# Other buffers for three leading MLP units, row-by-row differences of the activations, and block operands loaded product by product

## The chip, the cores and the metric

The program runs on one core of one Trainium2 chip. The metric is the device time of one launch in microseconds (us); the time of a kernel is the median of its runs. Before the change these were 3104.14, 3098.87 and 3105.69 us, median 3104.14 us. One more execution, taken by the hardware profiler, supplies every row shown here.

## The reference, cut to what matters

The network has two layers over 1024 latent tokens and 256 context tokens of 1024 channels in float32. Each layer has a mixer and then a squared-ReLU MLP, both under a modulated RMS norm:

```python
def squared_relu_mlp(h, w1, w2):
    return jnp.square(jax.nn.relu(h @ w1)) @ w2

x = x + mod_l[5] * squared_relu_mlp(modulate(rmsnorm(x, g_norm[l, 1]), mod_l[3], mod_l[4]), w_ff1[l], w_ff2[l])
return rmsnorm(x, g_final)
```

Only the MLP of the second layer is touched: `h` is 1024 tokens by 1024 channels, `w1` is 1024 by 4096, `w2` is 4096 by 1024. The context tokens have left the computation by then.

## The kernel before, in words

Precision first. A float32 operand is split into a high part `hi` (a cast on ACT, the scalar engine) and a low part `lo = v - hi` (a subtraction on DVE, the vector engine). A product is three matmuls, hi·hi, hi·lo and lo·hi, into one PSUM bank. So each 128x512 operand needs one ACT cast and one DVE subtraction before PE, the tensor engine, can use it. `osplit` (L1208 to L1217) makes the pair for an activation; L1265 and L1266 make it for a weight.

Both matmuls of this MLP are done by a seven-product scheme of the Strassen-Winograd kind. The operands are cut into 2 by 2 blocks, the blocks are added and subtracted, and seven products, named "1" to "7", take the place of eight. One **unit** computes a 2 by 2 group of 128x512 output tiles. The order of the products in a unit is `WORDER = ("1", "5", "6", "3", "7", "2", "4")`.

A unit has three PSUM banks (`BANK`, L1318): bank "a" (tag `acc`, 3 buffers) takes products 1, 6, 7 and 4 one on top of the other; bank "b" (tag `bd`, 4 buffers) takes 5 and then 3; bank "d" (also tag `bd`) takes 2. Between two products that accumulate in one bank, the running sum has to be copied out, because each of the four output tiles wants a different partial sum. So product 6 may start only when ACT has copied bank "a" after product 1 (`keep("11")`, line L1367), and product 7 only when the sum after 6 is copied (`keep("12")`). Product 2's bank is read by `plus("11")` (DVE, L1374, then ReLU and square on ACT, L1376 and L1377), which needs `keep("11")` done.

The up half (`h @ w1`): 16 units. The first three, `lead`, are **leading units** (`early=True`). Their products 1 and 2 need only the first 512 tokens, and run while the output projection of the mixer still finishes the other 512. Products 5, 6, 3, 7 and 4 need differences between the two halves of the tokens or the channels. These are made in `right1` (L1230 to L1251) once the norm of the second half is known. Then the five products are run for the three units together, one 128-row step of the inner dimension after the other (`together`). The twelve units 3 to 14 follow one by one, and unit 15 in another order.

The buffers around this: tag `x`, 8 buffers of 128x512, holds the residual stream of the first half, `x[k, 0]`, until `right1` has read it, and the output tiles of the units. `right1` releases its `x[k, 0]` of the lower channels only in its last loop (L1249, L1250), which forms the operand of product 4. Tag `t`, 5 buffers, holds sums of squares and temporaries. Tag `o`, 21 buffers, holds 16 operand tiles of products 6 and 7 throughout the up half, and on top of them `hi` parts on their way to DRAM. After a unit, `store` forms the right operands of the down half (differences of its four tiles) and writes them to `sw` in DRAM.

The down half (`... @ w2`): the hidden dimension is taken in five blocks, `DBLK`, of 2, 3, 3, 3 and 3 pairs of rows. Per block four units (`fo` = 0, 2, 4, 6), so with a 3-pair block a unit is 7 products x 3 steps x 3 matmuls = 63 matmuls, with the 2-pair block 42. The right operands of a block are loaded from `sw` by `down_ops` (L1419 on): 18 transfers of 256 KB straight into `hi` and `lo` tiles for products 1, 5 and 6 of a 3-pair block (L1430, tag `a5`, 32 buffers), and 12 into `t` tiles for 3, 7, 2 and 4 (L1433), which ACT and DVE then split into tiles of tag `a5` (product 3) or `o` (7, 2, 4). The left operands, weights, come per unit through staging tiles `st` (3 buffers) and `ws` (1 buffer), L1306, and are split by L1265 and L1266: first those of 1 and 2 (when the unit is made), then those of 5 and 6, of 3, and of 7 and 4 (when the unit meets product 5). Each result is added to the residual stream on DVE (L1442).

All transfers named here are issued by the SP queue, in order. The order of the instructions on each engine isn't written by hand: a scheduler runs through the program in a model of the chip, and at each moment gives an engine the ready instruction that comes first in program order (those under `tc.high_priority()` before). Readiness includes a free buffer. On the chip the order is fixed, and an engine waits at the head of its list.

Of the kernel before, what the change touches and what calls it, by code (L numbers as in the profile page):

```python
# [9 lines left out]
F32 = mybir.dt.float32  # L10
F32R = mybir.dt.float32r
# [6 lines left out]
P = 128  # L18
D = 1024
KT = D // P  # L20
# [31 lines left out]
def trunk(tc, es, A, out):  # L52
# [12 lines left out]
    def f(ap):  # L65
        return ap.bitcast(F32)
# [1141 lines left out]
    def osplit(pl, tag, bufs, v, b=None):  # L1208

        hi, lo = (pl.tile([P, 512], F32R, tag=tag, bufs=bufs, name=tag) for _ in range(2))  # L1210
        if b is None:
            act.copy(hi, v)
            dve.tensor_sub(lo, v, f(hi))
        else:
            act.activation(hi, v, AF.Identity, bias=b)
            dve.scalar_tensor_tensor(lo, v, b, f(hi), ADD, SUB)
        return hi, lo  # L1217
# [6 lines left out]
    def shift(k):  # L1224
        return mod[:, 1, 3, k, 0:1]
# [6 lines left out]
    def right1(r):  # L1232

        x, d = res.x, {}
        for k in range(HK):
            scaled(k, 1, r)
            dve.tensor_sub(x[k, 0], x[k, 1], x[k, 0])
        B["5"] = [osplit(ap_, "a5", 32, x[k, 0]) for k in range(HK)]
        for k in range(HK):
            scaled(k + HK, 1, r)  # L1240
            dve.tensor_sub(x[k, 0], x[k + HK, 1], x[k, 0])
        B["6"] = [osplit(po_, "o", NO, x[k, 0], shift(k + HK)) for k in range(HK)]
        B["3"] = [osplit(ap_, "a5", 32, x[k + HK, 1], shift(k + HK)) for k in range(HK)]
        db = pf.tile([P, 16], F32, name="db")[:, 0:HK]
        dve.tensor_sub(db, mod[:, 1, 3, HK:KT, 0], mod[:, 1, 3, 0:HK, 0])
        for k in range(HK):
            dve.tensor_sub(x[k, 1], x[k + HK, 1], x[k, 1])
        B["7"] = [osplit(po_, "o", NO, x[k, 1], db[:, k:k + 1]) for k in range(HK)]
        for k in range(HK):  # L1249
            dve.tensor_sub(x[k + HK, 0], x[k + HK, 0], x[k, 0])  # L1250
        B["4"] = [osplit(ap_, "a2", 8, x[k + HK, 0]) for k in range(HK)]  # L1251

    def left(load, n, early=False):
# [104 lines left out]
    def up_unit(j, early=False, order=WORDER):  # L1358

        t = {}  # L1360

        def e(n):
            t[n] = f(px.tile([P, 512], F32, tag="x", bufs=8, name="x"))
            return t[n]

        def keep(n):
            return lambda ps: act.copy(e(n), ps)  # L1367

        def square(n):
            dve.scalar_tensor_tensor(t[n], t[n], 0.0, t[n], MAX, MUL)  # L1370

        def plus(n):
            def g(ps):
                dve.tensor_add(t[n], t[n], ps)  # L1374
                if n == "11":
                    act.activation(t[n], t[n], AF.Relu)  # L1376
                    act.activation(t[n], t[n], AF.Square)  # L1377
                else:
                    square(n)
            return g  # L1380

        def last(ps):
            act.activation(e("21"), ps, AF.Relu)

        x5, x7 = (plus, keep) if order is LORDER else (keep, plus)
        done = {"1": keep("11"), "5": x5("22"), "6": keep("12"), "3": plus("12"), "7": x7("22"), "2": plus("11"),
                "4": last}
        u = Unit(up_left(j, early), done, B)

        def store():  # L1390
            act.activation(t["21"], t["21"], AF.Square)
            if j >= NWP:
                for n in ("11", "12", "21", "22"):
                    sp.dma_start(sd[2 * (j - NWP) + int(n[0]) - 1, int(n[1]) - 1], t[n])
                return

            def new(a, b):
                v = px.tile([P, 512], F32, tag="t", bufs=5, name="t")
                dve.tensor_sub(v, a, b)
                return v  # L1400

            o = {"1": t["11"], "2": t["21"], "3": t["22"]}
            o["5"] = new(t["12"], t["11"])
            o["6"] = new(t["22"], o["5"])
            dve.tensor_sub(t["12"], t["22"], t["12"])
            o["7"] = t["12"]
            o["4"] = new(t["21"], o["6"])
            for i, op in enumerate(WORDER):
                v = o[op]
                if i < NSPLIT:  # L1410
                    hi = po_.tile([P, 512], F32R, tag="o", bufs=NO, name="o")
                    act.copy(hi, v)
                    sp.dma_start(f(sw[j, i, 0]), f(hi))
                    dve.tensor_sub(v, v, f(hi))
                sp.dma_start(f(sw[j, i, 1]), v)
        u.store = store
        return u
# [84 lines left out]
    for i, blk in enumerate(DBLK):  # L1502
        right, nxt = nxt, {}
        for fo in range(0, KT, 2):
            if i or fo:
                d = down_unit(blk, fo, right)
            if i == 0 and fo < KT - 2:
                reload_x(fo + 2)
            if fo == KT - 2 and i + 1 < len(DBLK):
                nxt = down_ops(DBLK[i + 1])  # L1510
            d.run(*WORDER)
    s4, w4 = {}, []
    for hd in range(4):
        w4.append(wload(A["ff2"][1, 2 * NWP + hd], (1024,), *((None, "wa") if hd % 2 else (pfw, "wb"))))
# [103 lines left out]
```

## Time and profile before

| | before |
|---|---|
| median of the runs | 3104.14 us (3098.87 to 3105.69) |
| the profiled execution's own time | 3095.96 us |
| its span | 3094.2 us |
| PE busy, share of the span | 2933.4 us, 95% |
| DVE, ACT busy | 1959.3 us (63%), 1205.1 us (39%) |
| PE busy in 2400 to 2500 us, in 2700 to 2800 us | 79.64 and 89.24 of 100 us |
| mean granted TensorE clock of the span | 0.981 of full speed |

Where nothing else is said, times in the text are us from the start of the span. The MLP of the second layer takes the span from about 2400 us to its end; its down half begins at about 2740 us. [...]

### The profile page before, as it was taken

To read this page: it belongs to the slowest core of one execution; us is meant where nothing else is said; L and a number is where in the kernel's file an instruction comes from. 1 tells how busy PE (TensorE), PEld (TensorE's weight loads), DVE (VectorE), ACT (ScalarE), POOL (GpSimd) and SP (SyncE) were. 2 spreads that over 40 slices of the span, in tenths; PEclk is the share of its full clock that TensorE was granted. 3 is DMA by queue.
4 is the path that set the end of the run, shared out by engine and by line. 5 is a ranking of instruction groups with operands and counts; after the bars stand their busy time and mean duration, and the time that the engine had idled before them with its cause. 6 is when DMAs were issued, how large, how long until landed. Compare 5 with 4: busy or idle time off the path is not lost.

```text
span 3094.2 us, 44658 instructions
## 1 busy us (share of the span) xinstructions
PE 2933.4 (95%) x16386; PEld 2461.5 (80%) x16386; DVE 1959.3 (63%) x3885; ACT 1205.1 (39%) x2660; POOL 306.0 (10%) x483
## 2 busy tenths in 40 slices
PE   6899999999999999999999799999999799989998
PEld 5787878788888888888888677877877578867787
DVE  6859696646456544544446788567567776657666
ACT  3335354433321222222233145566666454433332
POOL 0002011001122222222100000000000000000000
PEclk9999999999999999999999899999999899999999
DMA  6143334551244444444321333232613386697751
GB/s 214 45 155 108 111 115 136 175 180 55 96 150 158 157 151 141 170 157 164 129 83 63 112 108 109 80 89 82 197 60 109 110 275 233 231 306 236 240 178 65
DMA packets 303803, 443.52 MB, mean 143 GB/s; under 512 B 25712, under 2 KB 174816, under 8 KB 303584
## 3 DMA queue, kind: packets, MB, share of 16 engines
q1 hardware_dynamic: 300992, 436.74, 43.4%
q10 hardware_dynamic: 2592, 3.93, 0.4%
q8 instruction: 129, 2.11, 0.3%
q14 instruction: 90, 0.74, 0.1%
HBM read 330.08 MB, written 110.49 MB: 142 GB/s over the span
## 4 chain that ended last, share of the span: by engine, by line
PE 73%; DVE 11%; DMA 9%; POOL 2%; ACT 2%; issue 2%; SPq 1%; POOLq 0%; DVEq 0%; ACTq 0%
PE acc L131 11%; PE acc L129 11%; PE acc L130 11%; PE acc L1314 8%; PE bd L1314 6%; PE ff L129 4%; PE ff L130 4%; PE ff L131 4%; PE po L1112 3%; PE S L1086 3%; DMA st<-in_ff_dram 2%; DMA kd<-rh 2%; PE pT L1107 2%; DMA qd<-rh 1%; DMA t<-sw 1%
## 5 line engine op out<-in xcount | busy, mean ns | idle before, releaser
L129 PE MATMUL acc<-a,wah 128*128 128x512 f32 (+1 forms) x1752 | 650.1, 371 | 22.4 <-DVE rt L1038 14.1
L130 PE MATMUL acc<-a,wah 128*128 128x512 f32 (+1 forms) x1752 | 644.6, 368 | 0.0
L131 PE MATMUL acc<-a,wal 128*128 128x512 f32 (+1 forms) x1752 | 643.4, 368 | 0.0
L129 PEld LDWEIGHTS acc<-a,wah 128*128 128x128 f32 x1752 | 336.0, 192 | 72.2 <-DVE rt L1038 14.7
L131 PEld LDWEIGHTS acc<-a,wal 128*128 128x128 f32 x1752 | 336.0, 192 | 47.5 <-DVE wal L111 0.6
L130 PEld LDWEIGHTS acc<-a,wah 128*128 128x128 f32 x1752 | 336.2, 192 | 45.6 <-issue 0.5
L110 ACT CAST wah<-st 128x1024 fp32r<-128x1024 f32 (+4 forms) x129 | 120.4, 935 | 483.2 <-DMA st<-in_ff_dram 375.1
L129 PE MATMUL ff<-s,wbh 128*128 128x512 f32 (+1 forms) x768 | 274.3, 359 | 0.2 <-DVE x L710 0.2
L130 PE MATMUL ff<-s,wbh 128*128 128x512 f32 (+1 forms) x768 | 272.4, 355 | 0.0
L131 PE MATMUL ff<-s,wbl 128*128 128x512 f32 (+1 forms) x768 | 271.6, 354 | 0.0
L111 DVE TENSOR_TENSOR wal<-st,wah 128x1024 fp32r<-128x1024 f32 (+4 forms) x129 | 139.3, 1083 | 202.9 <-ACT wah L110 202.6
L710 DVE SCALAR_TENSOR_TENSOR x<-ff,mod,x 128x512 f32<-128x512 f32 (+1 forms) x264 | 171.0, 658 | 96.1 <-PE ff L131 94.8
L1088 DVE TENSOR_REDUCE mx<-S 128x1 f32<-128x512 f32 (+1 forms) x288 | 165.6, 594 | 68.8 <-PE S L1086 67.3
L1094 ACT ACTIVATE p<-S,nm 128x512 f32<-128x512 f32 (+1 forms) x288 | 176.0, 620 | 45.7 <-DVE nm L1091 45.4
L1086 PE MATMUL S<-K,Q 128*128 128x512 f32 (+1 forms) x576 | 164.6, 386 | 15.7 <-ACT p L1094 7.1
L753 DVE TENSOR_TENSOR s<-s,s 128x512 fp32r<-128x512 f32 (+1 forms) x96 | 64.7, 680 | 167.9 <-ACT s L752 167.8
L1314 PE MATMUL bd<-a,wbh 128*128 128x512 f32 x480 | 153.9, 401 | 15.6 <-ACT wbh L1265 8.5
L129 PE MATMUL acc<-wah,a 128*128 128x256 f32 (+1 forms) x560 | 161.8, 290 | 6.5 <-ACT a L271 4.1
L129 PEld LDWEIGHTS ff<-s,wbh 128*128 128x128 f32 x768 | 144.8, 189 | 24.5 <-DVE x L710 1.0
L130 PEld LDWEIGHTS ff<-s,wbh 128*128 128x128 f32 x768 | 145.2, 189 | 20.7 <-DVE s L753 0.6
L131 PEld LDWEIGHTS ff<-s,wbl 128*128 128x128 f32 x768 | 144.9, 189 | 20.8
L131 PE MATMUL acc<-wah,a 128*128 128x256 f32 (+1 forms) x560 | 159.6, 290 | 0.3 <-DVE a L272 0.2
(391 smaller groups left out, 5913.1 us busy)
## 6 DMA issues: line engine op xcount, KB each, us to landing
st<-in_ff_dram SPq DMA_DIRECT2D x168, 256.0 KB
st<-in_ff_dram SPq DMA_DIRECT2D x68, 512.0 KB
st<-in_w_mod_dram SPq DMA_DIRECT2D x48, 512.0 KB
a<-sw SPq DMA_DIRECT2D x84, 256.0 KB
stm<-in_w_mod_dram SPq DMA_DIRECT2D x128, 128.0 KB
su<-st SPq DMA_DIRECT2D x32, 512.0 KB
bc<-rb SPq DMA_DIRECT2D x30, 512.0 KB
sv<-st SPq DMA_DIRECT2D x28, 512.0 KB
```

Of the source, the lines that this page charges most:

```text
L110: act.copy(hi, v)
L111: dve.tensor_sub(lo, v, f(hi))
L129: pe.matmul(ps, lh, rh, start=first, stop=False)
L130: pe.matmul(ps, lh, rl, start=False, stop=False)
L131: pe.matmul(ps, ll, rh, start=False, stop=last)
L710: dve.scalar_tensor_tensor(xt, ps, mod[:, self.l, ch, fo, s:s + 1], xt, MUL, ADD)
L753: dve.tensor_sub(lo, r, f(hi))
L1086: pe.matmul(s_, Q[m][:, kind, qb * P:(qb + 1) * P], K[hh, m][:, a:a + n], start=(kind == 0), stop=(kind == 1))
L1088: dve.tensor_reduce(mx[:, i:i + 1], s_, AX, MAX)
L1094: act.activation(e[:, a:a + n], S[i], AF.Exp, bias=nm, accum_out=Z[:, m, i:i + 1])
L1112: pe.matmul(po[:, 0:P], aT[:, (c - c0) * P:(c - c0 + 1) * P], v[c][:, hh * P:(hh + 1) * P], start=(c == 0), stop=(c == NCH - 1))
L1314: pe.matmul(ps, l_, r_, start=bool(first) and j == 0 and i == 0, stop=j == n - 1 and i == 2, skip_group_check=True)
```

## The change

Three things, in the order of the diff. In `right1`, the subtraction that forms the operand of product 4 for row `k` (old L1250) is put right behind the making and the split of that row's operand of product 6, in one loop. In `up_unit`, a leading unit puts the copy of product 1 ("11") into a `t` buffer and the copy of product 5 ("22") into an `o` buffer; "12" and "21", and all tiles of later units, stay in `x`. In the main loop, at the last unit of each block but the last, the remaining weights of that unit are asked for first, then the first unit of the next block is made and all its weights are asked for, and then the products run one by one, each followed by the loads of the next block's right operand for the same product; before, all loads of the next block stood ahead of the whole last unit. The number of computing instructions and of transfers is the same.

```diff
@@ -1239,15 +1239,14 @@
         for k in range(HK):
             scaled(k + HK, 1, r)
             dve.tensor_sub(x[k, 0], x[k + HK, 1], x[k, 0])
-        B["6"] = [osplit(po_, "o", NO, x[k, 0], shift(k + HK)) for k in range(HK)]
+            B["6"] = B.get("6", []) + [osplit(po_, "o", NO, x[k, 0], shift(k + HK))]
+            dve.tensor_sub(x[k + HK, 0], x[k + HK, 0], x[k, 0])
...
-        for k in range(HK):
-            dve.tensor_sub(x[k + HK, 0], x[k + HK, 0], x[k, 0])
         B["4"] = [osplit(ap_, "a2", 8, x[k + HK, 0]) for k in range(HK)]
@@ -1360,7 +1359,12 @@
         def e(n):
-            t[n] = f(px.tile([P, 512], F32, tag="x", bufs=8, name="x"))
+            if early and n == "11":
+                t[n] = px.tile([P, 512], F32, tag="t", bufs=5, name="t")
+            elif early and n == "22":
+                t[n] = f(po_.tile([P, 512], F32R, tag="o", bufs=NO, name="o"))
+            else:
+                t[n] = f(px.tile([P, 512], F32, tag="x", bufs=8, name="x"))
             return t[n]
@@ -1502,13 +1506,21 @@
         for fo in range(0, KT, 2):
-            if i or fo:
+            if fo:
                 d = down_unit(blk, fo, right)
...
-            if fo == KT - 2 and i + 1 < len(DBLK):
-                nxt = down_ops(DBLK[i + 1])
-            d.run(*WORDER)
+            last = fo == KT - 2 and i + 1 < len(DBLK)
+            if last:
+                next(d.left)
+                dn = down_unit(DBLK[i + 1], 0, nxt)
+                next(dn.left)
+            for op in WORDER:
+                d.run(op)
+                if last:
+                    nxt.update(down_ops(DBLK[i + 1], (op,)))
+            if last:
+                d = dn
```

## Rows read from the trace of the kernel before

**Rows 1.** The page: busy time of each engine (share of the span, instructions), and the chain of work that ended last, by engine.

```profile
PE 2933.4 (95%) x16386; PEld 2461.5 (80%) x16386; DVE 1959.3 (63%) x3885; ACT 1205.1 (39%) x2660; POOL 306.0 (10%) x483
...
PE 73%; DVE 11%; DMA 9%; POOL 2%; ACT 2%; issue 2%; SPq 1%; POOLq 0%; DVEq 0%; ACTq 0%
```

**Rows 2.** Busy time by stretch: bounds and length in us, then busy us and number of instructions of PE, PE's weight loads, DVE, ACT and POOL, then the granted TensorE clock, the share of the 16 DMA engines and GB/s.

```profile
2400.00:2500.00 100.00, 79.64 (x311) 59.76 (x311) 73.08 (x114) 47.73 (x77) 1.02 (x1) 0.88 0.44 142
2700.00:2800.00 100.00, 89.24 (x376) 70.93 (x375) 59.78 (x88) 38.89 (x65) 0.00 (x0) 0.95 0.88 290
```

**Rows 3.** PE in order of time around the five products of the leading units: start, length, line, output and inputs, and in brackets the idle time before and what ended it.

```profile
2429.72 0.65 PE L1314 MATMUL bd<-a,wbh 128*128 128x512 f32 x1 [2.75 <-ACT a L1212]
2432.79 0.80 PE L1314 MATMUL bd<-a,wbh 128*128 128x512 f32 x1 [2.42 <-DVE a L1213]
...
2449.29 1.22 PE L1314 MATMUL acc<-o,wbh 128*128 128x512 f32 x2 [11.88 <-ACT x L1367]
...
2482.73 0.73 PE L1314 MATMUL acc<-o,wah 128*128 128x512 f32 x2 [1.00 <-ACT x L1367]
```

**Rows 4.** Busy time by stretch (columns as in rows 2) of the same place.

```profile
2432.80:2437.40 4.60, 4.60 (x11) 3.06 (x11) 4.60 (x8) 1.64 (x3) 0.00 (x0) 0.57 0.00 0
2437.40:2449.30 11.90, 0.02 (x2) 0.01 (x1) 11.90 (x20) 6.19 (x11) 0.00 (x0) 0.62 0.00 0
2449.30:2454.10 4.80, 4.80 (x11) 3.26 (x12) 4.80 (x9) 4.62 (x9) 0.00 (x0) 0.53 0.02 5
2454.10:2465.40 11.30, 11.30 (x51) 9.24 (x50) 4.46 (x7) 5.70 (x12) 0.00 (x0) 1.00 0.18 46
```

**Rows 5.** DVE in order of time in `right1`.

```profile
2432.05 0.68 DVE L1213 TENSOR_TENSOR a<-x,a 128x512 fp32r<-128x512 f32 x1
...
2443.48 0.74 DVE L1216 SCALAR_TENSOR_TENSOR o<-x,mod,o 128x512 fp32r<-128x512 f32 x1
...
2447.88 0.68 DVE L1250 TENSOR_TENSOR x<-x 128x512 f32<-128x512 f32 x1
...
2449.74 0.68 DVE L1374 TENSOR_TENSOR x<-x,bd 128x512 f32<-128x512 f32 x1
```

**Rows 6.** ACT in order of time at the same place, with the last square of the norm's sum ahead of it.

```profile
2420.51 0.63 ACT L212 ACTIVATE t<-a 128x512 f32<-128x512 f32 x1
...
2448.65 0.58 ACT L1367 COPY x<-acc 128x512 f32<-128x512 f32 x1 [1.18 <-DVE x L1250]
...
2450.46 0.63 ACT L1376 ACTIVATE x<-x 128x512 f32<-128x512 f32 x1
```

**Rows 7.** PE in order of time in the down half, the rows that begin with an idle time: one from the last unit of the first block, three from the first two units of the second block, and four at the later changes of block.

```profile
2783.49 1.22 PE L1314 MATMUL bd<-a,wbh 128*128 128x512 f32 x2 [8.47 <-ACT wbh L1265]
...
2794.35 0.73 PE L1314 MATMUL acc<-o,wah 128*128 128x512 f32 x2 [0.83 <-DVE a L1442]
...
2802.23 0.70 PE L1314 MATMUL bd<-a,wbh 128*128 128x512 f32 x2 [0.52 <-DVE a L1442]
...
2815.91 0.73 PE L1314 MATMUL acc<-a,wbh 128*128 128x512 f32 x2 [1.01 <-DVE x L1442]
...
2876.85 0.73 PE L1314 MATMUL bd<-a,wbh 128*128 128x512 f32 x2 [0.67 <-DVE a L1442]
...
2919.17 0.72 PE L1314 MATMUL acc<-a,wbh 128*128 128x512 f32 x2 [0.85 <-DVE x L1442]
...
2936.83 0.74 PE L1314 MATMUL bd<-a,wbh 128*128 128x512 f32 x2 [0.76 <-DVE a L1442]
...
2987.85 0.71 PE L1314 MATMUL acc<-o,wah 128*128 128x512 f32 x2 [0.96 <-DVE a L1442]
```

**Rows 8.** Busy time by stretch (columns as in rows 2): after the gap at the first change of block, and one undisturbed unit of the second block.

```profile
2783.50:2788.40 4.90, 4.90 (x12) 3.81 (x13) 3.54 (x6) 2.92 (x6) 0.00 (x0) 0.51 0.91 286
...
2826.30:2840.70 14.40, 14.40 (x64) 11.84 (x64) 8.32 (x11) 3.04 (x5) 0.00 (x0) 1.00 0.34 96
```

**Rows 9.** The SP queue in order of time at the first change of block: start and length of a run of issues, line, destination and source, number of transfers.

```profile
2758.57 9.53 SPq L1430 DMA_DIRECT2D a<-sw  x16
2768.41 0.32 SPq L1433 DMA_DIRECT2D t<-sw  x1
2774.12 0.79 SPq L1430 DMA_DIRECT2D a<-sw  x2
2774.97 2.32 SPq L1433 DMA_DIRECT2D t<-sw  x5
2777.33 1.09 SPq L1306 DMA_DIRECT2D ws<-sv  x2
```

**Rows 10.** ACT in order of time there.

```profile
2774.82 0.62 ACT L1212 CAST a<-t 128x512 fp32r<-128x512 f32 x1 [10.37 <-PE acc L1314]
2780.56 2.00 ACT L1212 CAST o<-t 128x512 fp32r<-128x512 f32 x3 [5.12 <-DMA t<-sw]
2782.82 0.62 ACT L1265 CAST wbh<-ws 128x512 fp32r<-128x512 f32 x1 [0.26 <-DMA ws<-sv]
```

**Rows 11.** Busy time by stretch (columns as in rows 2) while the operands of the second block arrive.

```profile
2758.50:2768.30 9.80, 9.80 (x44) 8.02 (x44) 7.51 (x12) 2.17 (x4) 0.00 (x0) 1.00 1.01 343
2758.50:2783.10 24.60, 16.52 (x72) 13.17 (x71) 14.36 (x21) 4.92 (x9) 0.00 (x0) 0.90 0.86 296
2783.10:2795.50 12.40, 11.18 (x37) 8.41 (x38) 9.29 (x16) 6.41 (x12) 0.00 (x0) 0.79 0.96 284
```

## The prediction

> **What bounds the kernel.** I read the page first, then busy time by stretch, then PE's own order of time in the weak stretches, then ACT, DVE and SP there. PE is busy 95% of the span and makes 73% of the chain that ended last [rows 1]: with the number of matmuls unchanged, only PE's idle time and the time at its lower clock can be won. The change touches the second MLP, so the question is how much of either lies there. Two stretches of 100 us stand out: 2400 to 2500 us with 79.6 us of PE and a clock of 0.88, and 2700 to 2800 us with 89.2 us and 0.95 [rows 2]. In the first, PE waits 2.75 us, 2.42 us and then 11.88 us around the products 5 and 6 of the leading units [rows 3]; in the second it waits 8.47 us once, within the last unit of the first block [rows 7]. After both waits the clock is at its lower level for 4.8 to 4.9 us [rows 4, 8]. These two places are what the change can win; at the three later changes of block only four waits of 0.67 to 0.96 us are left [rows 7].
>
> As the unit of work I use 14.40 us for the 63 matmuls of an undisturbed unit [rows 8], 0.2286 us each.
>
> **Part 1: the leading units.** The 11.88 us end with the copy L1367 on ACT, `keep("11")` [rows 3], and this copy had waited for DVE's L1250 [rows 6], the last loop of `right1`, at 2447.88 us [rows 5]. So: product 1 stands in its bank, the copy needs an `x` buffer, all eight hold the residual stream, and the first one comes free with L1250. Product 6 may not accumulate before the copy; and product 5 of the second and third unit finds no `bd` bank, since product 2 sits in three of the four until `plus("11")`, DVE's L1374 at 2449.74 us, has run [rows 5].
>
> With "11" in `t` and "22" in `o`, copy, sum, ReLU and square run as soon as product 2 is done, before the norm. Then product 5 of all three units can follow the first rows, which are ready at 2432.05 us and after [rows 5], and PE goes on where it now stops at 2437.40 us [rows 4]. What is late next? The five products are 5 x 36 = 180 matmuls for the three units. Eleven are done by 2437.40 us [rows 4]; the other 25 of product 5 take 25 x 0.2286 = 5.7 us, to 2443.1. Product 6 takes its fourth row 27 matmuls later, at 2449.3. DVE now finishes that row at 2443.48 + 0.74 = 2444.2 us [rows 5]. The four subtractions moved ahead of it cost at most 4 x 0.68 = 2.7 us, so 2446.9: in time by 2.4 us. Without this cover the whole 2.7 us would be PE's. The copies of "12" need three `x` buffers when product 6 ends, about 2451.3; in the new order they come free row by row by then. Left where it is, the loop gives its first buffer at 2447.88 + 0.68 us [rows 5] and the others behind it, with the splits of product 7 between them: for the third buffer that is, as an estimate, 1 to 2 us too late. The reordering by itself is worth no more. Product 3, 7 and 4 come 8.2 us apart, their rows behind DVE work that the same queue does earlier than PE needs it.
>
> So 11.88 us go. The second start at the lower clock goes as well: 11 matmuls took 4.80 us [rows 4] where 11 x 0.2286 = 2.51 would do, 2.29 us. The wait of 1.00 us at 2482.73 us [rows 3] is again for an `x` buffer; the three units ask for 6 of the 8 in place of 12, so I let it go. The 2.75 and 2.42 us stay, they wait for the split of the first row.
>
> [...]
>
> Costs. Three copies of 0.58 us and six ReLUs and squares of 0.63 us [rows 6] move ahead of the norm on ACT, and DVE's three sums with them. ACT has idle time there (48 of 100 us busy [rows 2]), but a trio just ahead of the last square of the norm's sum [rows 6] would delay everything by 0.58 + 2 x 0.63 = 1.84 us. The squares now have one `t` buffer left of five, so each waits for the addition before it, at most 0.63 us more. Between 0 and 2.5 us, I take 0.5, near the idle end. In `store`, `o` has 21 - 16 - 3 = 2 buffers for high parts in place of 5, and three `t` are held. The cover is that "11" can be stored early and that unit 3 runs four products before it needs an `x` back; without it I bound the price by three waits of the 1.00 us kind, 3 us, and take 0.
>
> Part 1: -11.88 - 2.29 - 1.00 + 0.5 = -14.7 us.
>
> **Part 2: changes of block.** The 8.47 us end with the cast of weights of products 5 and 6 [rows 7]. Their transfer (`ws`) was issued at 2777.33 us, behind 18 + 6 loads of the next block [rows 9]: 16 went out at once, then SP stood from 2768.7 to 2774.1 us at a load whose `a5` buffer the last unit's own product 1 had to free, and five `t` loads went first as well. ACT was in the same position: a cast of a next-block operand waited 10.37 us, another three 5.12 us, with the weight cast behind them [rows 10]. With the unit's weights asked for before the block's operands, `ws` goes out when its buffer is free, well before 2774. Then the gap goes, and with it the slow restart: 12 matmuls in 4.90 us [rows 8] in place of 2.74, 2.16 us.
>
> What is late next is the operands themselves. Product 1 of the last unit ends at 2774.9; the other six are 36 matmuls, 8.2 us, so the next block starts at 2783.1 and its product 4, the last, at 2783.1 + 54 x 0.2286 = 2795.4. Until that time the DMA engines now move 24.6 x 296 + 12.4 x 284 = 10.8 MB from 2758.5 on [rows 11]; at the best rate seen, 343 GB/s, that is 31.5 us, to 2790.0. It fits by 5.4 us, and part of it is for later units. But twelve operands pass through five `t` buffers, and SP and ACT are in order. So some waiting comes back: between 0 and the whole 8.47 us. I take two waits of the mean length at later changes, 2 x 3.24 / 4 = 1.6 us [rows 7]. The waits of 0.83, 0.52 and 1.01 us behind the gap I leave.
>
> At the three later changes weights get ahead of operands too, but the four waits there, 3.24 us, are for DVE, and nothing says that they end: 0, with 3.24 either way. The gain could only come from the queue, and the queue isn't late there.
>
> Part 2: -8.47 - 2.16 + 1.6 = -9.0 us.
>
> **The sum.** -14.7 - 9.0 = -23.7 us. The profiled execution took 3095.96 us (span 3094.2, 1.8 us around it), so 3072.3 us for such an execution. It lies 8.2 us below the median shown, 3104.14; the change is to be seen against the median, so I forecast 3104.14 - 23.7 = 3080.4 us.
>
> **Rivals.** (a) Only the first stall goes: the block's operands are late in place of the weights, and the 8.47 us come back under another name. For it: the DMA engines are 86% and 96% busy there [rows 11]. Against: the 5.4 us of room. 3104.14 - 14.7 = 3089.4 us.
>
> (b) Only the second goes: DVE is busy for the whole 11.9 us of the first gap [rows 4], so PE could wait for rows of operands in place of banks. Against: rows of product 6 done at 2444.2 us. 3104.14 - 9.0 = 3095.1 us.
>
> (c) Slower: at the later changes a cast of an operand, whose buffer only the last unit's product frees, now stands on ACT right between the last unit's products and ahead of weight casts of the next unit. That is the mechanism of the 5.12 us in rows 10, at three places where it doesn't stop PE now. At the full price of the first change, 8.47 + 2.16 = 10.63 us each, it costs 31.9 us against 23.7: 3112.3 us. It decides from 7.9 us per change on. Against it: today's order puts these loads even earlier, and PE isn't stopped there.
>
> [...]
>
> (d) Nothing: the order on the engines comes from a planner that goes by readiness, and both stalls return with the same releasers. 3104 us. Against: in the first the buffer itself changes; in the second it is priority that decides between ready loads.
>
> **Chances and range.** Forecast 0.66, (a) 0.14, (b) 0.10, (c) 0.05, (d) 0.05. The forecast's own range is 3069 to 3088 us: with every wait named above gone (3.24 + 2.36 + the 1.6 and 0.5 I gave back, 7.7 us) and a median at the lowest of the runs shown it would be near 3068; with 2.5 + 3 + 2.7 us of uncovered cost, 3088. With (a) and most of (b): 3068 to 3097 us. About 0.2% (6.2 us) is what a measurement of this kernel can tell from no change. Faster by more: 0.66 + 0.14 and half of (b), 0.85; within: the rest of (b) and (d), 0.10; slower: 0.05.
>
> **What would show it.** Right: no idle time over 1 us between 2433 and 2460 us, L1367 of the leading units before the norm's reciprocal, the clock at its lower level once there; the five products done near 2476 us; `ws` issued ahead of most loads of the second block, no gap in the last unit of the first block. Wrong: PE waiting for L1216 or L1213 in product 6 (rival b), for a `t` cast in product 3, 7, 2 or 4 of the second block (a), gaps over 2 us at the later changes (c), or the old releasers with the old lengths (d).

## The result, and the profile after

The changed kernel takes 3079.69 us (median of 4 runs, 3076.41 to 3087.28) against 3103.01 us for the kernel before, run beside it. The ratio is 0.9928, with a 95% interval of 0.9909 to 0.9947: faster by 23.3 us, where 23.7 us were forecast. The two parts did not come out as forecast, though: the leads gave less and the changes of block more, and the two errors nearly cancel.

Up to the leads' first copies, at about 2394 us, PE, ACT and DVE run the same instructions in the same order in both programs, and still the leads' first landmark, the broadcast of the norm (L232), starts at 2425.84 us before and at 2431.91 us after. In the experiments below it lies between 2428.7 and 2439.0 us. So single profiles are compared over stretches that begin there:

- the **lead stretch**, from L232 to the ReLU of "21" of unit 7: before 163.79 us, after 153.24 us, 10.55 us less;
- from there to the 8th residual update of the down half: 166.63 and 166.80 us, no change;
- the **block stretch**, from that 8th update to the end of the span: before 337.94 us, after 322.75 us, 15.19 us less.

Of the kernel before, busy time by stretch (columns as in [rows 2]): the lead stretch, then the block stretch cut at the 28th update, which stands at the end of the first block.

```profile
2425.84:2589.63 163.79, 145.49 (x607) 115.41 (x608) 115.97 (x166) 81.00 (x127) 0.00 (x0) 0.94 0.57 195
...
2756.26:2796.35 40.09, 29.99 (x118) 23.41 (x119) 26.50 (x41) 11.70 (x21) 0.00 (x0) 0.87 0.89 290
2796.35:3094.20 297.85, 282.03 (x1315) 231.67 (x1313) 200.04 (x307) 86.96 (x135) 2.61 (x3) 0.99 0.56 176
```

The same of the kernel after, and the two stretches of [rows 2]:

```profile
2431.91:2585.15 153.24, 145.21 (x607) 115.36 (x608) 114.73 (x164) 77.56 (x121) 0.00 (x0) 0.97 0.60 208
...
2751.95:2780.08 28.13, 26.77 (x115) 21.38 (x116) 21.81 (x33) 6.83 (x12) 0.00 (x0) 1.00 0.90 283
2780.08:3074.70 294.62, 281.52 (x1318) 232.63 (x1316) 204.59 (x314) 91.85 (x144) 2.62 (x3) 0.98 0.60 190
...
2400.00:2500.00 100.00, 87.92 (x353) 65.97 (x352) 82.50 (x127) 52.89 (x86) 1.03 (x1) 0.95 0.50 172
2700.00:2800.00 100.00, 97.08 (x415) 76.52 (x414) 67.00 (x99) 39.69 (x66) 0.00 (x0) 1.00 0.92 298
```

Length minus PE's busy time is PE's idle time. With the number of matmuls equal (607; 1433 in the block stretch) a difference in busy time is one of time per matmul, and where the granted clock differs it is put down to the clock: in the kernel before a matmul takes 0.44 and 0.41 us in the two restarts (granted clock 0.53 and 0.51 [rows 4, 8]) and 0.23 us at 1.00 [rows 8]. The lower clock or level is a granted clock of 0.50: of the 160 windows of 0.25 us from 2430 to 2470 us of the kernel before, 77 show 1.00, 80 show 0.50 and 3 a number between. In the leads idle time fell from 18.30 to 8.03 us, and busy time by 0.28 us alone. In the block stretch idle time fell from 10.10 + 15.82 = 25.92 to 1.36 + 13.10 = 14.46 us, and busy time by 3.73 us.

PE in order of time, of the kernel after: the idle rows of the leads, which answer to [rows 3], with the first row of product 3 and the last matmul of the leading units' product 4 between them, and then all idle times over 0.5 us from 2740 us to the norm at the end, which answer to [rows 7].

```profile
2435.78 1.04 PE L1313 MATMUL bd<-a,wbh 128*128 128x512 f32 x3 [2.75 <-ACT a L1212]
2438.86 0.80 PE L1313 MATMUL bd<-a,wbh 128*128 128x512 f32 x1 [2.04 <-DVE a L1213]
2458.65 1.29 PE L1313 MATMUL acc<-o,wah 128*128 128x512 f32 x3 [1.64 <-ACT o L1215]
...
2463.98 0.62 PE L1313 MATMUL bd<-a,wbh 128*128 128x512 f32 x2
...
2485.37 0.39 PE L1313 MATMUL acc<-a,wal 128*128 128x512 f32 x1
...
2518.55 0.73 PE L1313 MATMUL acc<-o,wah 128*128 128x512 f32 x2 [1.49 <-ACT wah L1264]
...
2752.75 0.73 PE L1313 MATMUL acc<-a,wbh 128*128 128x512 f32 x2 [0.89 <-DVE x L1446]
2772.95 0.73 PE L1313 MATMUL acc<-a,wbh 128*128 128x512 f32 x2 [0.56 <-DVE x L1446]
2796.33 0.50 PE L1313 MATMUL acc<-o,wah 128*128 128x512 f32 x1 [0.70 <-ACT o L1212]
2824.23 0.73 PE L1313 MATMUL acc<-o,wah 128*128 128x512 f32 x2 [1.22 <-DVE a L1446]
```

The 11.88 and the 8.47 us are gone, and so is the 1.00 us for an `x` buffer. New are the 1.64 us ahead of product 7, for a cast on ACT, and 1.49 us in a later unit, for a weight cast. PE's order is another one, too: before, product 7 comes behind product 3; now its first 13 matmuls (from 2458.65 us) stand ahead of product 3 (from 2463.98 us). The four waits at the later changes of block are gone too.

The page after shows PE at 96% of the span and 76% of the chain, where [rows 1] has 95% and 73%:

```profile
PE 2937.0 (96%) x16386; PEld 2466.6 (80%) x16386; DVE 1960.1 (64%) x3885; ACT 1206.1 (39%) x2660; POOL 303.4 (10%) x483
...
PE 76%; DVE 9%; DMA 8%; ACT 2%; POOL 2%; issue 1%; SPq 0%; POOLq 0%; DVEq 0%; ACTq 0%
```

### The profile page after: what moved, and what is told of

Same layout as the page of the kernel before. It is cut to its first block, busy times and chain, and to the rows that moved or that the text cites. A ratio compares the mean times of both kernels' runs of the same rounds, so it can differ in the third digit from the quotient of the medians.

```text
span 3074.7 us, 44664 instructions
## 1 busy us (share of the span) xinstructions
PE 2937.0 (96%) x16386; PEld 2466.6 (80%) x16386; DVE 1960.1 (64%) x3885; ACT 1206.1 (39%) x2660; POOL 303.4 (10%) x483
## 4 chain that ended last, share of the span: by engine, by line
PE 76%; DVE 9%; DMA 8%; ACT 2%; POOL 2%; issue 1%; SPq 0%; POOLq 0%; DVEq 0%; ACTq 0%
PE acc L129 11%; PE acc L131 11%; PE acc L130 11%; PE acc L1313 9%; PE bd L1313 7%; PE ff L129 4%; PE ff L130 4%; PE ff L131 4%; PE po L1112 3%; PE S L1086 3%; DMA kd<-rh 2%; DMA st<-in_ff_dram 2%; PE pT L1107 2%; DMA qd<-rh 1%; POOL rs L661 1%
## 5 line engine op out<-in xcount | busy, mean ns | idle before, releaser
L130 PE MATMUL acc<-wal,a 128*128 128x256 f32 (+1 forms) x560 | 161.4, 289 | 0.0
```

What stands on the lines that cost most here:

```text
L130: pe.matmul(ps, lh, rl, start=False, stop=False)
```

## The experiments

The twelve runs in one table, beside before and after. Ratio is against runs of the kernel before on the same chip. Lead and block are the two stretches of each profile; idle is the lead stretch minus PE's busy time.

| kernel | median us | ratio (95%) | lead | idle | block |
|---|---|---|---|---|---|
| before | 3103.01 | | 163.79 | 18.30 | 337.94 |
| after | 3079.69 | 0.9928 (0.9909 to 0.9947) | 153.24 | 8.03 | 322.75 |
| after, once more | 3077.87 | 0.9917 (0.9903 to 0.9931) | 153.92 | 8.91 | 322.08 |
| row order alone | 3097.25 | 0.9982 (0.9970 to 0.9993) | 156.77 | 11.98 | 336.19 |
| buffers alone | 3090.81 | 0.9958 (0.9944 to 0.9973) | 151.32 | 7.90 | 337.07 |
| only "11" elsewhere | 3092.87 | 0.9966 (0.9953 to 0.9979) | 154.65 | 8.74 | 337.05 |
| row order and buffers | 3093.80 | 0.9966 (0.9953 to 0.9979) | 152.35 | 7.49 | 336.64 |
| block loop alone | 3087.08 | 0.9953 (0.9938 to 0.9969) | 163.44 | 18.09 | 321.87 |
| after, weights ahead only | 3077.18 | 0.9923 (0.9909 to 0.9937) | 153.18 | 8.58 | 322.25 |
| after, products only | 3090.78 | 0.9957 (0.9944 to 0.9970) | 153.28 | 8.09 | 332.69 |
| after, product 3's weights first | 3087.56 | 0.9957 (0.9944 to 0.9969) | 167.00 | 17.88 | 321.90 |
| buffers and block loop | 3075.79 | 0.9912 (0.9899 to 0.9925) | 151.00 | 7.82 | 323.23 |
| after, differences late | 3076.10 | 0.9909 (0.9898 to 0.9921) | 150.34 | 6.83 | 324.18 |
| buffers, block loop, product 7 first | 3081.03 | 0.9917 (0.9901 to 0.9934) | 152.32 | 8.50 | 321.89 |

Kernels with the same code in a stretch agree there within 1.6 us in the leads and 2.3 us in the blocks, where the medians carry the scatter of all 3080 us.

### The parts alone

**Row order alone** (the new loop of `right1`, nothing else):

```diff
-        B["6"] = [osplit(po_, "o", NO, x[k, 0], shift(k + HK)) for k in range(HK)]
+            B["6"] = B.get("6", []) + [osplit(po_, "o", NO, x[k, 0], shift(k + HK))]
+            dve.tensor_sub(x[k + HK, 0], x[k + HK, 0], x[k, 0])
...
-        for k in range(HK):
-            dve.tensor_sub(x[k + HK, 0], x[k + HK, 0], x[k, 0])
```

> The kernel before with the row order alone (the products' activation differences made row by row; nothing else changed). Three stretches of the profile are compared, since the first 200 us scatter by several us from run to run: (i) the norm broadcast (L232) to the relu of product 21 of unit 7, before 163.8, after 153.2; (ii) the 8th to the 28th residual update of block 0, before 40.1, after 28.1; (iii) the 28th update to the end of the span, before 297.9, after 294.6. Theory 1 (the buffers do the work; the order only frees the x rows earlier, as the prediction said, worth 1 to 2 us): (i) 161 to 164, the idle time in front of product 1's copy still over 8 us, (ii) and (iii) as before. Rival (the order does it, since product 1's copy waits for an x row that the order frees some 10 us earlier): (i) 156 or less, the 11.88 us stall under 4. Total by theory 1: 3101 to 3103; by the rival 3095.

The rival held, nearly: 7.0 us less in the leads, and the 11.88 us gone. Of this kernel, ACT's first copy of "11", and then the two longest idle rows of PE behind the norm's rows:

```profile
2441.84 0.59 ACT L1366 COPY x<-acc 128x512 f32<-128x512 f32 x1 [1.13 <-DVE o L1216]
```

```profile
2458.57 0.73 PE L1313 MATMUL bd<-a,wbh 128*128 128x512 f32 x2 [1.56 <-ACT x L1366]
...
2460.77 0.50 PE L1313 MATMUL bd<-a,wbl 128*128 128x512 f32 x1 [1.47 <-DVE wbl L1265]
```

Counted from L232 the copy comes at 11.75 us, and at 22.81 us before [rows 6]: the order alone frees the first `x` buffer 11 us earlier. What stays are shorter waits: 1.56 us for a copy to `x`, and 1.47 us for the low part of a weight of product 3.

**Buffers alone** ("11" to `t`, "22" to `o`), and **only "11"** (without the `elif`); the rest goes to `x` as before:

```diff
+            if early and n == "11":
+                t[n] = px.tile([P, 512], F32, tag="t", bufs=5, name="t")
+            elif early and n == "22":
+                t[n] = f(po_.tile([P, 512], F32R, tag="o", bufs=NO, name="o"))
...
```

> The kernel before with the buffers alone (in the leading units the copy of product 11 goes to a t buffer and that of 22 to an o buffer; row order and block changes as before). Theory 1 (the buffers take the stall away; the changed row order is what leaves 1.64 us of idle and a second slow stretch in the kernel after): (i) 149 to 152, so better than the 153.2 of the kernel after; 11.88 us stall gone, no stretch below 0.9 granted clock behind 2455. Rival (the order is needed too, because the split of product 3's weights and not the rows is late): (i) 153 to 157. Stretches (ii) and (iii) as before, 40 and 298. Total by theory 1: 3089 to 3091, by the rival 3093 to 3096.

> The kernel before with one buffer alone: in the leading units the copy of product 11 goes to a t buffer, that of 22 stays in an x buffer; rows and blocks as before. Theory 1 (the 11.88 us are the copy of 11 waiting for an x buffer, and 22 comes late enough to find one): (i), norm broadcast L232 to the relu of unit 7's product 21, 151 to 153, within 1.5 of the run with both buffers (151.3). Rival (22 then waits for the same x rows in its place): (i) 155 to 160, with a new idle of 3 us or more that ends on a copy to x.

With both buffers theory 1 held: 151.32 us, shorter than the kernel after. With "11" alone the result lies between the two bands: two waits for copies to `x` appear, 1.33 and 1.37 us, and behind them the clock is at its lower level (0.50). PE and a stretch of this kernel:

```profile
2459.16 0.73 PE L1314 MATMUL bd<-a,wbh 128*128 128x512 f32 x2 [1.33 <-ACT x L1370]
2462.26 1.22 PE L1314 MATMUL acc<-o,wah 128*128 128x512 f32 x2 [1.37 <-ACT x L1370]
```

```profile
2462.26:2467.26 5.00, 5.00 (x12) 3.95 (x13) 4.48 (x7) 3.10 (x6) 0.00 (x0) 0.50 0.66 196
```

So "11" does 9.1 us of the 12.5, and moving "22" the other 3.3 (154.65 - 151.32).

**Row order and buffers:**

> The kernel before with row order and buffers, without the new loop over the down blocks. Theory 1 (the parts are independent): (i) 153.2 as in the kernel after, (ii) 40.1 and (iii) 297.9 as before, total 10.5 us below the kernel before, 3092.5. Rival (the first profile of the kernel after was an unlucky one for stretch (i), since how long the second slow stretch lasts varies): (i) about 149, total 3088.

152.35 us, nearer to theory 1's 153.2 than to the rival's 149, and 1.0 us longer than with the buffers alone. The two edits overlap (7.0 and 12.5 us alone, 11.4 us together): both remove the same wait.

**Block loop alone:**

> The kernel before with the new loop over the down blocks alone (first weights of the next block ahead, its operands product by product; leading units as before). Theory 1 (the two parts are independent): (i) 163.8 as before, (ii) 28, (iii) 294.6, so the total 15 us below the kernel before, 3088. Rival (part of the gain in the later block changes was run-to-run scatter of the one profile): (iii) 297 to 298 and the total 3091.

Theory 1 held: the leads as before, the block stretch 16.1 us shorter, the median 16.4 us lower. The rival did not: from the 28th update to the end it is 294.26 us against 297.85, so the gain behind the first change of block, 3.2 us in the profile of the kernel after, is no scatter of one profile.

### Which half of the block loop

```diff
-            for op in WORDER:
-                d.run(op)
-                if last:
-                    nxt.update(down_ops(DBLK[i + 1], (op,)))
+                nxt.update(down_ops(DBLK[i + 1]))
+            d.run(*WORDER)
```

> The kernel after, but the next block's operands are loaded in one go behind its first unit's weights, and not product by product. Theory 1 (the 8.47 us stall was the first unit's weights behind 20 operand transfers, so the weights ahead take it away alone): (ii) 8th to 28th residual update 28 to 29 and (iii) 294.6 to 296, total within 2 us of the kernel after. Rival (the product-by-product order of the operands is what does it): (ii) 34 to 40, since the operands' casts then crowd ScalarE's queue in the block's last unit; total 6 to 12 above the kernel after.

And the other half alone: the three lines that ask for the unit's own remaining weights, make the next block's first unit and ask for its weights, all ahead of the products, are taken out, and the loads stay product by product.

```diff
             if last:
-                next(d.left)
-                dn = down_unit(DBLK[i + 1], 0, nxt)
-                next(dn.left)
+                pass
...
```

> The kernel after with the operands of the next down block loaded product by product, but its first unit's weights where the kernel before has them (behind all operand loads). Theory 1 (the weights ahead do all of it; the run with the weights ahead alone gave 27.8 in stretch (ii), 8th to 28th residual update): (ii) 36 to 40, the stall of about 8 us at the block's end is back, and (iii), 28th update to the end, 296 to 298; total 10 to 14 above the kernel after, about 3090. Rival (either half is enough, since operands loaded product by product leave room in the queue for the weights): (ii) 28 to 31 and the total within 3 us of the kernel after.

The weights ahead do it alone: 322.25 us, as with both. The products alone leave 332.69 us and a median of 3090.78, as theory 1 said; the stall was not in the stretch that it named (27.0 us from the 8th to the 28th update, not 36 to 40), but just behind the 28th update, in the second block's first unit. In the last unit of the first block its own `ws` now go out behind 6 operand loads, at 2762.25 us, and PE doesn't stop there. Of the kernel with the products alone: PE, the SP queue, and one stretch.

```profile
2789.35 1.22 PE L1313 MATMUL acc<-a,wah 128*128 128x512 f32 x2 [5.38 <-ACT wah L1264]
```

```profile
2765.75 9.88 SPq L1434 DMA_DIRECT2D a<-sw  x12
2775.68 7.28 SPq L1437 DMA_DIRECT2D t<-sw  x6
...
2784.78 0.44 SPq L1305 DMA_DIRECT2D st<-in_ff_dram  x1
...
2789.13 0.96 SPq L1305 DMA_DIRECT2D ws<-sv  x2
```

```profile
2788.00:2792.00 4.00, 2.65 (x6) 1.87 (x7) 2.98 (x4) 2.69 (x5) 0.00 (x0) 0.50 0.93 332
```

Weights (`st`, `ws`) again stand behind operands, now the weights of the next block's first unit, with 5.38 us of idle time and a slow restart (granted clock 0.50). In the kernel after, SP issues two pairs of `ws` loads among the first operands, 5.3 and 10.3 us behind the 8th update, where the pair of [rows 9] comes 21.1 us behind it:

```profile
2757.22 0.88 SPq L1305 DMA_DIRECT2D ws<-sv  x2
...
2762.24 0.96 SPq L1305 DMA_DIRECT2D ws<-sv  x2
```

### What the row order costs beside the buffers

Three kernels of one comparison: the weight split of product 3 put first in the planner's order, the old row order with buffers and loop, and the kernel after once more.

```diff
-            act.copy(hi, v)
-            dve.tensor_sub(lo, v, f(hi))
+            with tc.high_priority() if early and qs == ("S4",) else nullcontext():
+                act.copy(hi, v)
+                dve.tensor_sub(lo, v, f(hi))
```

> The kernel after, with the split of product 3's weights (casts and subtractions of the leading units) put ahead of product 6's copies in the instruction order; buffers, rows and block loop as in the kernel after. Theory 1 (in the kernel after, product 3 comes late because on ScalarE, which works in order, two of its weight casts stand behind product 6's three copies and product 7's row casts): no idle of 1.64 us and no fall of the clock behind 2455, stretch (i) (norm broadcast L232 to the relu of unit 7's product 21) 150 to 151.5 against 153.2, total about 2 us below the kernel after. Rival (what is late are the rows of product 7, which come from VectorE, and the changed row order has put them late): (i) 153 again, the idle still ends on the o casts of L1215.

> The kernel before with the buffers and the new block loop, but the old row order. Theory 1 (the parts add up, and the new row order costs 1 to 2 us once the buffers are changed, as the two runs with and without it said: (i) 151.3 against 152.4): (i) 151.3, (ii) 27.6 to 28.1, (iii) 294.3 to 294.6; total 3103.5 minus 12.7 minus 16.4, 3074.4, against 3079.7 for the kernel after. Rival (the difference of the row order was scatter, or the parts don't add): total within 2 us of the kernel after.

> The kernel after once more, beside the two others on one chip. Expected 3077 to 3082; (i) 152.3 to 153.2 with 1.6 us of idle and a lower clock near 2455 again (theory 1), or, if that was an accident of one execution, (i) 149 to 151 without them.

My theory 1 of the first of these fell. The wait ahead of product 7 grew to 2.16 us and still ended on the `o` casts, as the rival said. Its 153 us did not come either, but 167.00 us, since the priority did harm elsewhere: two `ws` loads that SP issues together at 2476.52 us in the kernel after stood between the stores to `sw` until 2504.42 and 2512.46 us, and PE waited 9.60 us. SP in the kernel after, then PE, SP and ACT of the kernel with product 3's weights first:

```profile
2476.52 0.82 SPq L1293 DMA_DIRECT2D ws<-su  x2
```

```profile
2457.70 0.74 PE L1314 MATMUL acc<-o,wah 128*128 128x512 f32 x2 [2.16 <-ACT o L1215]
...
2518.80 1.22 PE L1314 MATMUL bd<-a,wbh 128*128 128x512 f32 x2 [9.60 <-ACT wbh L1265]
```

```profile
2504.42 0.45 SPq L1294 DMA_DIRECT2D ws<-su  x1
...
2512.46 0.64 SPq L1294 DMA_DIRECT2D ws<-su  x1
```

```profile
2517.70 1.04 ACT L1265 CAST wbh<-ws 128x1024 fp32r<-128x1024 f32 x1 [7.88 <-DMA ws<-su]
```

The kernel after once more showed the 1.64 us again, ending on the same cast, and 153.92 us; its clock stayed at 1.00 there (last section). The old order with buffers and loop gave 151.00 us in the leads, as theory 1 had it. Its median (3075.79) can't be told from that of the kernel after in the same comparison (3077.87): the intervals overlap. The next kernel takes back half of the row order, the four differences:

```diff
             B["6"] = B.get("6", []) + [osplit(po_, "o", NO, x[k, 0], shift(k + HK))]
-            dve.tensor_sub(x[k + HK, 0], x[k + HK, 0], x[k, 0])
...
         B["7"] = [osplit(po_, "o", NO, x[k, 1], db[:, k:k + 1]) for k in range(HK)]
+        for k in range(HK):
+            dve.tensor_sub(x[k + HK, 0], x[k + HK, 0], x[k, 0])
```

> The kernel after, with the four differences x[k+4,0] - x[k,0] back at their old place behind product 7's rows; product 6's rows stay row by row with their differences. Theory 2 (the five traces with row order and buffers together all show an idle of 1.64 or 2.16 before product 7 that ends on its o casts, and a lower clock behind it; the two with the buffers alone show neither. The four differences of 0.68 put product 7's rows 2.5 us later on VectorE, so their casts fall behind a weight cast and three copies on ScalarE): (i) 151.0 to 151.5, no lower clock behind product 7, as in the run without the row order. Rival (it is the interleaving of product 6's rows that does it): (i) 153 to 154 with 1.6 us of idle and the lower clock.

150.34 us, 0.7 us below theory 2's band, and a granted clock of 1.00 behind the wait: theory 2 held, it is the moved differences. (Of the five traces that the expectation names, three have the lower clock there: 0.72 over 6 us in the kernel after and in row order and buffers, 0.50 over 5 us from 2461.16 us with product 3's weights first. Two, the kernel after once more and weights ahead only, show 1.00; see the last section.) How the differences cost is seen on ACT, in order of time; first the kernel after, then the one with the old order, buffers and loop.

```profile
2455.90 0.62 ACT L1264 CAST wbh<-st 128x512 fp32r<-128x512 f32 x1 [4.41 <-PE acc L1313]
2456.42 1.55 ACT L1371 COPY x<-acc 128x512 f32<-128x512 f32 x3
2457.86 0.74 ACT L1215 ACTIVATE o<-a,db 128x512 fp32r<-128x512 f32 x1
2458.48 0.63 ACT L1212 CAST a<-x 128x512 fp32r<-128x512 f32 x1
2458.99 0.74 ACT L1215 ACTIVATE o<-a,db 128x512 fp32r<-128x512 f32 x1
...
2460.12 0.63 ACT L1264 CAST wbh<-st 128x512 fp32r<-128x512 f32 x1
2460.64 0.73 ACT L1215 ACTIVATE o<-a,db 128x512 fp32r<-128x512 f32 x1
...
2461.78 0.72 ACT L1215 ACTIVATE o<-a,db 128x512 fp32r<-128x512 f32 x1
...
2464.34 0.65 ACT L1264 CAST wbh<-st 128x512 fp32r<-128x512 f32 x1
```

```profile
2452.56 0.73 ACT L1215 ACTIVATE o<-a,db 128x512 fp32r<-128x512 f32 x1 [3.94 <-DVE a L1247]
2456.34 0.62 ACT L1265 CAST wbh<-st 128x512 fp32r<-128x512 f32 x1 [3.06 <-PE acc L1314]
2456.87 0.72 ACT L1215 ACTIVATE o<-a,db 128x512 fp32r<-128x512 f32 x1
...
2458.00 0.72 ACT L1215 ACTIVATE o<-a,db 128x512 fp32r<-128x512 f32 x1
...
2460.09 0.73 ACT L1215 ACTIVATE o<-a,db 128x512 fp32r<-128x512 f32 x1
```

Product 7's four rows are the casts `o<-a,db`. From L232 they come at 25.95, 27.08, 28.73 and 29.87 us in the kernel after, and at 19.69, 24.00, 25.13 and 27.22 us with the old order. With product 4's differences made early, its casts (`a<-x`, L1212) are ready and stand between those of product 7. And the first `o` cast has fallen behind the weight cast, which waits 4.41 us for PE and product 6, until 2455.90 us, though the first row of its input (DVE's L1248, from 2453.28 us, 0.68 us each) was done by 2453.96 us: ACT took its list in order. Product 3's three weight casts (`wbh<-st`) are spread over 8.4 us in the kernel after, from 2455.90 to 2464.34 us, with casts of products 7 and 4 between; in the kernel before they stand at 2464.02 and 2465.50 us (two), and product 3 follows product 6 there without idle time.

The price of the moved differences is clearest in PE's time from the end of product 6 to the end of product 4: 28.6 to 28.8 us in the five profiles of kernels with row order and buffers (product 3's weights first left aside), 27.5 to 27.8 us in the three with the buffers and without the moved differences (buffers alone, buffers and block loop, differences late). Some more is lost by the later wait for a weight cast: 1.26 to 1.71 us in the five; 0.85, 1.01 and none over 0.3 us in the three. Why it is longer was not followed.

The last kernel puts product 7's casts ahead, with the old order, buffers and loop:

```diff
-        B["7"] = [osplit(po_, "o", NO, x[k, 1], db[:, k:k + 1]) for k in range(HK)]
+        with tc.high_priority():
+            B["7"] = [osplit(po_, "o", NO, x[k, 1], db[:, k:k + 1]) for k in range(HK)]
```

> The kernel with buffers and block loop but the old row order, with product 7's row casts put ahead of product 3's first weight casts and product 6's copies in ScalarE's order. Theory 2 (what is left of idle between products 6 and 7, 1.33 us, and the 0.79 before the first weights of product 3, is ScalarE's order): (i) 150 to 150.7 against 151.0, total 0 to 1 us below the kernel with buffers and blocks (3075.8), too little for the totals to tell; the idle before product 7 under 1.0. Rival (the idle ends on a copy that frees a psum bank and not on the casts): idle 1.3 again, (i) 151 or, where the weight casts get later, 152 to 153.

The rival held: the idle time before product 7 is 1.49 us and ends on a copy that empties a bank of product 6, and the stretch is no shorter (152.32 us). PE of this kernel:

```profile
2464.35 0.73 PE L1315 MATMUL acc<-o,wah 128*128 128x512 f32 x2 [1.49 <-ACT x L1373]
```

No kernel of these beats the kernel after by more than its runs scatter; those with the old order or with the differences late (151.00 and 150.34 us) are 2 to 3 us shorter in the leads than its 153.24 us.

## Why the prediction was right, and where it was not

**The total** was right by luck in part: -23.3 us measured and -23.7 us forecast, from terms that were off by 4 us one way and 6 us the other. (The two profiles differ by 10.55 + 15.19 - 0.17 = 25.6 us behind L232, the medians by 23.3; that is within the scatter of single runs.) Rivals (a) to (d) are out: both stalls went, and the later changes got faster, not slower. A small part of (b) came, PE waiting for rows of operands: the 1.64 us, in product 7 and not in product 6.

**Part 1: -14.7 forecast, -10.55 measured.** The 11.88 us went, and the copies ahead of the norm cost nothing where 0.5 us was set: from the last row of L1216 ahead of the norm to L232 it is 35.88 us before and 35.67 us after. Product 6 was fed in time, as worked out: no idle row stands between 2438.86 and 2458.65 us. It ended 1.64 us ahead of the latter, at 2457.0 us, where the forecast's 2451.3 us, moved by the 6.07 us of L232, gives 2457.4.

From there it failed. The step is "Product 3, 7 and 4 come 8.2 us apart, their rows behind DVE work that the same queue does earlier than PE needs it". It counted DVE and not ACT, which casts the same rows in the order of its list, between copies, weight casts and product 4's casts. And it took PE's order as 3, 7, 4, where PE takes a part of product 7 straight behind product 6; product 7 adds to the bank that product 6 has just filled, so the copy of that bank stands between. By the forecast the end of product 4 comes 24.7 us behind that of product 6; it came 28.75 us behind. 1 us of the 4 is the moved differences. The other 3 us stand in the kernels without them too, where PE waits 1.33 us for the copy of that bank and then 0.7 to 0.8 us for a weight cast of product 3 or 7; the rest of it was not taken apart. (The leading units' product 4 ends at 2485.8 us; the forecast's 2476, moved by 6.07, gives 2482.1.) Two of the prediction's own signs failed with it: an idle time over 1 us stands there, and the clock fell a second time (0.52 from 2461.90 to 2463.90 us).

The term for the second slow restart, 2.29 us, is right where product 7 is fed better: with buffers, block loop and old order PE's busy time is 145.49 - 143.18 = 2.31 us less, in the kernel after 0.28. The 1.00 us wait went, as set down; 1.49 us came in a later unit, for a weight cast that the sum did not have.

**The sentence "The reordering by itself is worth no more"** (than 1 to 2 us) was wrong twice: alone it is worth 7.0 us, since it frees the `x` buffers that the copy of "11" waits for, and beside the buffers it costs about 2 us (five profiles at 152.35 to 153.92 us, three without the moved differences at 150.34 to 151.32 us).

**Part 2: -9.0 forecast, -15.19 measured.** The mechanism at the first change was right. SP stood from 2768.73 to 2774.12 us at one load, with the `ws` loads behind it in its list [rows 9], while the `ws` buffer had been read for the last time by 2761.50 us (DVE's L1266, 0.68 us from 2760.82 us). The weights asked for ahead remove the gap by themselves, and loading product by product without them only moves it into the next unit. Three terms were mis-sized. Of the 1.6 us given back for late operands 0.70 us came, one wait for a cast of an operand. The three waits behind the gap, 2.36 us, and the four at the later changes, 3.24 us, were left as they were; of these 5.60 us 1.22 us stand in the second block, and no wait over 0.5 us behind it up to the norm at the end. That "nothing says that they end" and that "the queue isn't late there" was a reading that stopped at DVE. Of the kernel before, ACT and then DVE ahead of PE's wait at 2876.85 us [rows 7]:

```profile
2874.79 0.62 ACT L1212 CAST o<-t 128x512 fp32r<-128x512 f32 x1 [4.09 <-DMA t<-sw]
```

```profile
2875.44 0.69 DVE L1213 TENSOR_TENSOR o<-t,o 128x512 fp32r<-128x512 f32 x1 [2.56 <-ACT o L1212]
2876.05 0.74 DVE L1442 SCALAR_TENSOR_TENSOR a<-bd,mod,a 128x512 f32<-128x512 f32 x1
```

DVE's update that PE waits for stands behind the subtraction of a next block's operand, which waits for its cast on ACT, which waits for its load. PE had filled the bank of that update by 2874.14 us, when DVE stood idle; DVE took the subtraction first, at 2875.44 us. The other three waits have such a subtraction ahead of them as well (DVE idle 1.59 to 2.65 us). From the last update of the second block to that of the third, and on to that of the fourth, it takes 57.63 us each in the kernel after, without idle time on PE; before, 59.89 and 59.06 us.

Third, PE's busy time fell by 3.73 us, not by 2.16. Some 2.5 us of it lie up to the 28th update (29.99 and 26.77 us, with 3 matmuls fewer of 0.23 us after), the slow restart: that term was there, and a little larger. The other 1.2 us lie behind that update (282.03 and 281.52 us, with 3 matmuls more after). The granted clock there is 1.00 in both kernels up to the norm at the end (2796.35 to 3080 us before, 2780.08 to 3060 us after), so it isn't the clock; what it is was not found.

## What to carry to other kernels

A buffer that a copy waits for can be had by another pool or by freeing it earlier; do one, since here they removed the same wait (7.0 and 12.5 us alone, 11.4 us together), and a step made earlier pushed others back on ACT, which took its list in order (about 2 us). When an operand passes through two engines, work out its time on both: here, for product 7's first row, DVE's was in time (the input done by 2453.96 us) and ACT's was not (the cast began at 2457.86 us). A load that the next product needs goes into the queue ahead of those that a later block needs: 322.25 us in the block stretch with the weights ahead, 336.64 us without. A priority given to casts can push loads back, here two by 30 and 38 us counted from L232, so look at SP after each such change. When PE waits for DVE, look what DVE waited for (here 2.56 us for a cast, which had waited 4.09 us for its load).

## What the runs showed of the hardware that was not expected

The same code, with the same idle time of 1.64 us ahead of product 7, was followed by the lower clock in three profiles (the kernel after, row order and buffers, products only) and by the full clock in two (after once more, weights ahead only). Of each kind one, the stretch of 6 us from that row on, kernel after and kernel after once more:

```profile
2458.65:2464.65 6.00, 5.95 (x16) 3.61 (x17) 5.84 (x10) 6.00 (x12) 0.00 (x0) 0.72 0.10 38
```

```profile
2465.00:2471.00 6.00, 5.31 (x17) 2.91 (x18) 5.83 (x10) 6.00 (x12) 0.00 (x0) 1.00 0.10 32
```

It cost nothing: 16 matmuls at a clock of 0.72, and 17 at 1.00 with idle time between, since the rows came no faster either way (26 with the differences late). From the end of product 6 to the end of product 4 the three take 28.67 to 28.75 us and the two 28.63 and 28.69 us. So the low clock had no price of its own beside this late operand. Nor did idle time alone tell when the clock falls: with the row order alone 1.56 and 1.47 us stand close together and it stays at 1.00 (2456 to 2476 us), with only "11" moved 1.33 and 1.37 us are followed by 0.50. What decides was not settled.
